# Token mixing of one encoder layer in a new order on all engines, with some products in unsplit float32

## The chip, the cores and the metric

The kernel runs on one core of a Trainium2 chip: TensorE (matrix products into PSUM), VectorE (DVE in the profile), ScalarE (ACT), GpSimd (POOL), SyncE (SP, whose queue issues nearly all loads here), and 16 DMA engines that bring data from HBM into SBUF. The metric is device time in microseconds, the median of several runs; lower is better.

## What is computed

One layer for 256 tokens of width 1024, in float32:

```python
z = x @ w_in + b_in                        # 1024 -> 2304: pool 256, q, k, v 512 each, conv a, g 256 each
mix = concat(pool_mixer(z), neighbourhood_attention(z), conv_module(z)) @ w_out + b_out
x1 = layer_norm(ALPHA * x + mix, ln1_g, ln1_b)
logits = x1 @ w_router + b_router          # 32 experts, the top 4 of each token, softmax over them
for e in range(32):
    g = minimum(x1 @ w_gate[e] + b_gate[e], 7.0)
    u = clip(x1 @ w_up[e] + b_up[e], -7.0, 7.0)
    out += gates[:, e:e+1] * (((u + 1) * g * sigmoid(1.702 * g)) @ w_down[e] + b_down[e])
y = layer_norm(ALPHA * x1 + out, ln2_g, ln2_b)
```

The pool mixer takes centred means over 2, 4, 8 and 16 tokens; attention runs over a 4 by 64 grid in 2 x 16 query blocks with a learned bias; the conv module is GLU, a depthwise convolution of 31 taps, a layer norm over 256 channels, swish and a 256 x 256 product. Each expert has three 1024 x 1024 float32 matrices, 12.6 MB, so the expert weights are 403 MB.

## The kernel before, in words

Everything is one function, `encoder_layer`, in a schedule written out by hand: each engine executes its instructions in the order of the text, and semaphores for data and buffers are added by the framework. The loads go through one in-order queue (SP).

**Buffers.** 22 slots of 128 x 2048 float32 (1.05 MB), `slot(i, name)`; a tile in a slot waits until everything that used the tile before it is done. In token mixing they hold the input x transposed (slot 0), the raw input weights (`wi`), their split parts (`wp`), q and k, the attention scores (`sb`), W_out raw and split (`wo`). As they come free, `load_ahead` (line 307) fills them with expert 0's weights in the order of `places`, and in the loop over experts `load_expert(e + 1)` (line 895) loads the next expert's 12 pieces in the same cycle of 20 places. PSUM: four accumulator banks `acc` (2 halves of tokens x 2 halves of channels), three rotating banks `bk` and one `bg`.

**Split products.** A float32 operand is written as the sum of a rounded high part (`nc.scalar.copy` into float32r) and a low part (raw minus high, on VectorE, or on GpSimd where `eng=nc.gpsimd`), line 104. `zstep` (line 213) then makes three float32r products, high x high, high x low, low x high. `zproj` does this for 8 slices of the 1024 channels and four 128-column blocks: first the conv columns, then Q, K, pool, V.

**Order of token mixing.** Loads of x and the conv columns in eight pieces; conv, Q; the taps of the depthwise convolution (62 VectorE instructions, `run_taps`) fill VectorE's gaps; K; pool columns (`wi_p`); scores with mask and bias (lines 353 to 363: VectorE scales and adds, takes the maximum, negates it, ScalarE makes the exponentials); nine pooling steps on GpSimd (lines 328 to 336); V; normalisation of the scores (line 391); transposes of probabilities and V (415, 420), pool columns through their map (405), attention products (434). GpSimd also subtracts for half of V's split (107) and all four parts of W_out (299), adds the mask to the bias table (201), and splits the gate and up biases into three bfloat16 parts (470, 636).

**Output projection and norm 1.** `outproj(tt, kk)` (line 476) adds slice kk of the mix for token half tt to two accumulators, three split products each. Between them stand the conv module's layer norm (488 to 509; its two products with the reciprocal deviation are line 508), its pointwise product (520), and x times ALPHA plus b_out (501). Then norm 1 by token halves: `stats1` adds (572) and takes statistics, `ln_stats` ends in a power on GpSimd (551), `apply1` scales on VectorE (577), `turn1` transposes the normed rows and applies the gain (583, 561, 563), `router` multiplies by the router weights (598) and finds the top 8, `chosen` and `positions` make a mask and each token's place in its expert's list, `acc_start` (592) puts ALPHA times x1 into the four accumulators.

**Experts.** Each has 64 places. `gather` (716) picks its tokens with a 0/1 matrix (`slots_of`, 707) for two experts at a time, `first` (748) makes the gate and up products, `act_gate`, `act_up` (768) the activation, `turn` (778) transposes, `down` (801) the third product, `scatter` (813) adds the gated rows to the accumulators one expert later, `select` (695) prepares the scatter matrix. The fullest expert has more tokens than 64: `places_of` (984) exchanges its column with that of expert `FULL` = 16 in small tables (`exchange`, 999 to 1008, six times), and at `e == FULL` a second block of 32 places is computed (`block`, with the gather of line 727). The order of expert weights is read at run time from `whose`. After expert 31 the second norm is done and stored.

## Time and profile before

| | us |
|---|---|
| median of 3 runs | 1088.27 (1087.99 to 1088.78) |
| the profiled execution | 1080.62 |
| its span, first to last instruction | 1078.4 |
| TensorE busy in the span | 975.7 (90%) |
| VectorE | 333.4 (31%) |
| ScalarE | 167.6 (16%) |
| GpSimd | 77.4 (7%) |
| DMA: bytes moved, mean rate | 422.99 MB, 392 GB/s |

A share over the whole span mixes the first 175 us, where the layer's first half runs, with 900 us of experts; the rows below are of single stages. A float32 product leaves two records of TensorE, a float32r or bfloat16 product or a transpose one. "PEclk" is the share of the full TensorE clock that was granted, 1.00 for 2.4 GHz and 0.50 for 1.2.

### The profile page before, as it was taken

Reading aid. Unit: us, or ns where it says so; the run is one execution under the profiler, and the core shown is the slowest. Engines: PE = TensorE matmul, PEld = TensorE weight load, DVE = VectorE, ACT = ScalarE, POOL = GpSimd, SP = SyncE. Lnnn points to the kernel's source line nnn. Section 1 sums busy time; section 2 is a strip of 40 time slices with the busy share of each in tenths; the row PEclk is TensorE's granted clock in tenths of the full one; section 3 lists DMA queues with packets and bytes.
Section 4 is the critical chain, followed back from the end, with each engine's and each line's share of the span. In section 5 each row is a group of like instructions: output and inputs, shape, how many; then the busy total and the mean of one; then the engine's idle time right before and its main releaser. Section 6 shows DMA issues by size and latency. Waiting matters only on the chain.

```text
span 1078.4 us, 13697 instructions
## 1 busy us (share of the span) xinstructions
PE 975.7 (90%) x5194; PEld 424.3 (39%) x5194; DVE 333.4 (31%) x795; ACT 167.6 (16%) x331; POOL 77.4 (7%) x40
## 2 busy tenths in 40 slices
PE   7968889999999999998989899999989898898985
PEld 6956734343434343433324343433223232323222
DVE  5999652222212322221221312222112121212114
ACT  5644411011101010100101110101001010101001
POOL 1894200000000000000000000000000000000001
PEclk9989889999999999999999999999999999999998
DMA  9674779999999999999999999999999999999994
GB/s 340 265 308 169 310 282 393 421 421 421 421 421 422 421 421 421 421 421 421 421 421 421 420 420 421 422 421 421 420 421 422 421 421 421 420 422 420 421 401 171
DMA packets 61768, 422.99 MB, mean 392 GB/s; under 512 B 6818, under 2 KB 7330, under 8 KB 11780
## 3 DMA queue, kind: packets, MB, share of 16 engines
q1 hardware_dynamic: 61348, 421.42, 95.2%
q8 instruction: 42, 0.69, 0.3%
q0 software_dynamic: 208, 0.40, 0.1%
q10 hardware_dynamic: 144, 0.26, 0.1%
q14 instruction: 26, 0.21, 0.0%
HBM read 421.01 MB, written 1.05 MB: 391 GB/s over the span
## 4 chain that ended last, share of the span: by engine, by line
DMA 69%; PE 19%; DVE 6%; issue 3%; POOL 1%; ACT 1%; SPq 0%; DVEq 0%; ACTq 0%; POOLq 0%
DMA w<-in_w_up_dram 23%; DMA w<-in_w_down_dram 23%; DMA w<-in_w_gate_dram 22%; PE bk L748 5%; PE bk L801 4%; PE bg L748 3%; PE bk L716 1%; DVE cacc L255 1%; DVE sb L391 1%; PE acc L482 1%; DVE more L508 1%; DMA wi<-in_w_in_dram 0%; PE bk L778 0%; PE acc L218 0%; ACT wp L106 0%
## 5 line engine op out<-in xcount | busy, mean ns | idle before, releaser
L748 PE MATMUL bk<-w,xgp 128*64 128x512 f32 x1024 | 240.2, 603 | 21.1 <-DMA w<-in_w_up_dram 21.0
L748 PE MATMUL bg<-w,xgp 128*64 128x512 f32 x1024 | 231.4, 595 | 17.6 <-DMA w<-in_w_gate_dram 17.6
L801 PE MATMUL bk<-w,aT 128*64 128x512 f32 (+1 forms) x1024 | 226.4, 598 | 1.2 <-DMA w<-in_w_down_dram 1.2
L748 PEld LDWEIGHTS bg<-w,xgp 128*64 128x64 f32 x1024 | 70.7, 136 | 167.5 <-issue 111.1
L748 PEld LDWEIGHTS bk<-w,xgp 128*64 128x64 f32 x1024 | 67.5, 137 | 162.9 <-issue 101.7
L801 PEld LDWEIGHTS bk<-w,aT 128*64 128x64 f32 (+1 forms) x1024 | 69.3, 136 | 135.7 <-issue 127.2
L806 DVE SCALAR_TENSOR_TENSOR y<-bk,gs,y 128x512 fp32r<-128x512 f32 x31 | 23.3, 751 | 272.9 <-ACT y L805 272.9
L757 DVE TENSOR_SCALAR g<-bg 128x512 f32<-128x512 f32 x32 | 22.1, 691 | 175.3 <-PE bg L748 175.3
...
L780 ACT COPY aT<-bk 128x256 f32<-128x256 f32 (+1 forms) x66 | 24.4, 369 | 262.0 <-PE bk L778 257.5
L758 ACT ACTIVATE s<-g 128x512 f32<-128x512 f32 (+1 forms) x33 | 20.6, 624 | 261.8 <-DVE g L757 261.8
L716 PE MATMUL bk<-se,xa 128*128 128x128 f32 x512 | 59.9, 275 | 0.0
L716 PEld LDWEIGHTS bk<-se,xa 128*128 128x128 f32 x512 | 58.4, 192 | 0.0
L768 DVE TENSOR_SCALAR u<-bk 128x256 f32<-128x256 f32 (+1 forms) x66 | 27.5, 417 | 95.6 <-PE bk L748 95.6
L805 ACT ACTIVATE y<-bk,gs 128x512 fp32r<-128x512 f32 x31 | 21.3, 687 | 214.3 <-PE bk L801 214.3
L813 PE MATMUL acc<-y,st 64*128 64x512 f32 x248 | 46.4, 447 | 1.1 <-ACT y L805 0.8
L778 PE MATMUL bk<-ident,g 128*128 128x128 f32 x128 | 27.7, 299 | 15.0 <-DVE g L769 14.1
L698 DVE TENSOR_SCALAR st<-bk 128x256 fp32r<-128x256 f32 x32 | 13.6, 425 | 81.2 <-PE bk L695 81.2
L216 PE MATMUL acc<-x,wp 128*128 128x256 f32 x96 | 29.1, 303 | 7.6 <-ACT wp L106 7.6
L561 ACT ACTIVATE xgp<-bk,g1b 128x128 f32<-128x128 f32 x64 | 24.1, 458 | 76.0 <-PE bk L716 76.0
L563 DVE TENSOR_SCALAR xgp<-bk,g1b 128x128 f32<-128x128 f32 x64 | 21.9, 404 | 44.1 <-PE bk L716 44.1
L218 PE MATMUL acc<-x,wp 128*128 128x256 f32 x96 | 29.1, 303 | 4.5 <-POOL wp L107 4.0
...
## 6 DMA issues: line engine op xcount, KB each, us to landing
...
w<-in_w_down_dram SPq DMA_DIRECT2D x124, 1024.0 KB, 19.8
wi<-in_w_in_dram SPq DMA_DIRECT2D x7, 1024.0 KB, 11.6
...
```

The lines of the kernel that those rows point to most:

```text
L216: nc.tensor.matmul(b[:, :256], w(0, k, j), xh[:, k, :], start=(k == 0), stop=False)
L218: nc.tensor.matmul(b[:, :256], w(1, k, j), xh[:, k, :], start=False, stop=(k == 7))
L561: nc.scalar.activation(o, i, AF.Identity, bias=b, scale=g)
L716: nc.tensor.matmul(p[:, i * 128:(i + 1) * 128], x1n[:, tt, (g + i) * 128:(g + i) * 128 + 128], se[:, tt, :], start=(tt == 0), stop=(tt == 1))
L748: nc.tensor.matmul(p[i * c:(i + 1) * c, :n], xg[:, k, :], w[k // 2][:, k % 2, i * n:(i + 1) * n], start=False, stop=(k == 7))
L757: nc.vector.tensor_scalar(g[:], p[:, :n], 7.0, None, op0=ALU.min)
L768: nc.vector.tensor_scalar(u[:, o], p[:, o], -7.0, 7.0, op0=ALU.max, op1=ALU.min)
L778: nc.tensor.transpose(p[:, j * 128:j * 128 + 128], a[:, j * 128:j * 128 + 128], ident[:])
L780: nc.scalar.copy(aT[:, o], p[:, :h * 256].rearrange("p (j n) -> p j n", n=128)[:, o])
L801: nc.tensor.matmul(p[o:o + c, :], aT[:, k % h, k // h * c:(k // h + 1) * c], rows_of(w, k, dh), start=(k == of_part[0]), stop=(k == of_par ...
L806: nc.vector.scalar_tensor_tensor(y[:, 1], p[:], gs[:], y[:, 0].bitcast(F32), op0=mult, op1=sub)
L813: nc.tensor.matmul(acc[tt][dh][:], st[dh * 64:dh * 64 + 64, tt, :], y[dh * 64:dh * 64 + 64, i, :], start=False, stop=False, skip_group_che ...
```

## The change

Token mixing is ordered anew:

- The conv columns and the pool columns of the input projection are float32 products from the raw weights (`zplain`, one float32 product instead of three float32r ones); Q, K and V stay split. So do W_out's slices 2 to 7, while its slices 0 and 1 (pool rows, `WHOLE`) are unsplit float32 products.
- All splits, the masks and the pooling steps run on VectorE. GpSimd keeps the broadcasts of bias rows, the powers of the layer norms, and the issue of twelve small loads within SBUF that put the three parts of the gate and up biases in place (`bias_parts`); the biases come as one array of 128 partitions. The negation of the maxima is made by the reduction. V's evacuation is all on ScalarE.
- Loads: x and the conv columns come in five pieces; slots are dealt out differently (`places`); x itself is loaded before the weights of expert 0.
- The router's products are made from the rows before norm 1 (`hT`, `scores`): router weights times the gain (`gw`), and mean and deviation of each row are applied to the 32 scores (`rsum`). Norm 1's scaling runs on ScalarE. The top-4 mask is made by one comparison and one reduction.
- ALPHA times x1 isn't put into the accumulators before the experts; `add_x1` adds one of its four quarters in each of the experts 4, 6, 10 and 12.
- Expert 0's tokens are gathered alone, expert 1's within expert 0's up product. Of the exchange of columns only `whose` is made before expert 0, the other tables after its up product. The exchanged place is expert 20 instead of 16.

The diff, cut to its core:

```diff
-FULL = 16
+FULL = 20
+X1_AT = (4, 6, 10, 12)
...
+    for t, src, o in ((xT, xT_d, slice(0, 2)), (wi_conv[0], w_in_at[1792], slice(0, 2)), (xT, xT_d, slice(2, 8)),
+                      (wi_conv[0], w_in_at[1792], slice(2, 4))):
+        nc.sync.dma_start(t[:, o, :], src[:, o, :])
+    nc.sync.dma_start(wi_conv[1], w_in_at[1792][:, 4:8, :])
...
-    wi_k = load_in(768, 512, (1, 2))
+    wi_k = load_in(768, 512, (13, 19))
+    wi_p = load_in(0, 256, (14,))
...
-    nc.gpsimd.dma_start(bgu[:, 0], b_gate)
-    nc.gpsimd.dma_start(bgu[:, 1], b_up)
-    nc.gpsimd.dma_start(small[32:33, :D], rows_d[:, :D])
-    nc.gpsimd.dma_start(small[64:65, :32], rows_d[:, D:D + 32])
-    nc.gpsimd.dma_start(bdn, b_down)
+    bgu = small[:, :512]
+    bparts = small[:, 512:1280].bitcast(BF16).rearrange("p (i f) -> p i f", i=3)
+    nc.sync.dma_start(bgu, b_gu)
+    brows = small[:, 1280:1792]
+    for i in range(2):
+        nc.sync.dma_start(brows[32 + 32 * i:33 + 32 * i, :], rows_d[:, i * 512:i * 512 + 512])
+    nc.sync.dma_start(brows[96:97, :32], rows_d[:, D:D + 32])
+    nc.sync.dma_start(bdn, b_down)
+    wi_v = load_in(1280, 512, (1, 2))
...
-        nc.gpsimd.tensor_tensor(biasT[:, pair, :, :124], biasT[:, pair, :, :124],
+        nc.vector.tensor_tensor(biasT[:, pair, :, :124], biasT[:, pair, :, :124],
...
+    def bias_parts():
+
+        for i in range(3):
+            if i:
+                nc.vector.tensor_tensor(bgu, bgu, bparts[:, i - 1], op=sub)
+            nc.scalar.copy(bparts[:, i], bgu)
+            for h in range(2):
+                for m in range(2):
+                    p = 64 * h + 32 * m
+                    nc.gpsimd.dma_start(bg3[32 * i:32 * i + 32, m, h * 512:h * 512 + 512], bparts[p:p + 32, i])
+
+    def zplain(raw, bs):
+
+        per = 8 // len(raw)
+        for k in range(8):
+            for j, b in enumerate(bs):
+                nc.tensor.matmul(b[:, :256], raw[k // per][:, k % per, j * 128:j * 128 + 128], xT[:, k, :],
+                                 start=(k == 0), stop=(k == 7))
...
+    zplain(wi_conv, bks)
+    act_table(AF.Sigmoid)
+    for i in range(0, 8, 4):
+        split(xT[:, i:i + 4], xh[:, i:i + 4], xl[:, i:i + 4])
     wp_q.add(wi_q[0], (9, 10))
     wp_q.add(wi_q[1], (11, 12))
-    wi_p = load_in(0, 256, (4,))
-    load_bias(1)
-    wi_v = load_in(1280, 512, (3,))
-    wi_v += load_in(1280, 512, (13,), 1)
-    bks = [acc[i // 2][i % 2] for i in range(4)]
-    act_table(AF.Sigmoid)
-    zproj(wp_c, bks)
+    qbs = [bank("bg" if j == 3 else "bk") for j in range(4)]
+    zproj(wp_q, qbs)
+    wp_k.add(wi_k[0], (5, 6))
...
-    NT = (4, 12, 3, 9, 16, 4, 3)
+    TAPS = (8, 10, 16, 8, 100, 14)
...
+    run_taps(TAPS[0])
+    wp_v.add(wi_v[0], (9, 10))
+    wp_v.add(wi_v[1], (11, 12))
+    run_taps(TAPS[5])
+    add_mask(1)
...
-    wo_raw = {k: load_rows(p, w_out, k) for k, p in ((1, 1), (2, 2), (0, 19), (3, 3))}
-    wo_places = ((0, 14), (5, 6), (7, 8), (11, 12))
+    bias_parts()
+    wo_raw = {k: load_rows(p, w_out, k) for k, p in ((1, 21), (0, 3), (2, 4), (3, 13))}
+    xa = slot(19, "xa")[:].rearrange("p (t d) -> p t d", t=2)
+    nc.sync.dma_start(xa, x_d.rearrange("p (t d) -> p t d", t=2))
+    WHOLE = (0,)
+    wo_places = ((5, 6), (7, 8), (1, 2), (9, 10))
     wo = {}
 
-    def split_out(k, eng=nc.gpsimd):
+    def split_out(k):
 
         hi, lo = [slot(p, f"wo{p}", F32R)[:].rearrange("p (k c) -> p k c", k=2) for p in wo_places[k]]
         wo[k] = hi, lo
-        nc.scalar.copy(hi, wo_raw[k])
-        return lambda: eng.tensor_tensor(lo, wo_raw[k], hi.bitcast(F32), op=sub)
-
-    places = (21, 13, 1, 9, 10, 15, 16, 2, 5, 6, 3, 7, 8, 0, 14, 11, 12, 18, 4, 17)
+        assert k not in WHOLE
+        split(wo_raw[k], hi, lo)
+
+    places = (5, 6, 0, 15, 16, 21, 4, 11, 12, 3, 13, 7, 8, 1, 2, 18, 14, 9, 10, 17)
...
+    zplain(wi_p, pbs)
...
-        nc.vector.tensor_reduce(mx[:, i0:i0 + 4], t, axis=AX.X, op=ALU.max)
-        nc.vector.tensor_scalar(mx[:, i0:i0 + 4], mx[:, i0:i0 + 4], -1.0, None, op0=mult)
+        nc.vector.tensor_reduce(mx[:, i0:i0 + 4], t, axis=AX.X, op=ALU.max, negate=True)
...
+    nc.vector.tensor_tensor(s2[:, :, 1:272], uT[:, :, 0:271], uT[:, :, 1:272], op=add)
+    nc.vector.tensor_tensor(s4[:, :, 1:271], s2[:, :, 0:270], s2[:, :, 2:272], op=add)
...
+    split_out(1)
+    split_out(2)
...
+        if kk // 2 in wo:
+            wh, wl = [w[:, kk % 2] for w in wo[kk // 2]]
+            ps = (mh, wh), (mh, wl), (ml, wh)
+            ps = [(a[:, kk], w) for a, w in ps]
+        else:
+            ps = [(more[:, kk // 6, kk % 2], wo_raw[kk // 2][:, kk % 2])]
...
+    run_taps(TAPS[2])
     pool_out()
+    load_ahead(5)
+    for tt in range(2):
+        outproj(tt, 0, first=True)
+    run_taps(TAPS[3])
...
+    split_out(3)
...
+    gw = pa.tile([128, 8, 64], F32, name="gw", tag="cacc")
+    rsum = pa.tile([128, 64], F32, name="rsum")
+    wr = par[:, P_WR:P_WR + 256].rearrange("p (k e) -> p k e", k=8)
+    for i, p in enumerate((P_G1, P_B1)):
+        nc.vector.tensor_tensor(gw[:, :, 32 * i:32 * i + 32], wr, par[:, p:p + 8, None].to_broadcast([128, 8, 32]), op=mult)
...
+            nc.scalar.activation(half(tt, dh), half(tt, dh), AF.Identity, bias=shift[:], scale=mv[:, 1:2])
...
+        nc.vector.scalar_tensor_tensor(lg[:], rsum[:, :32], mv[:, 0:1], b[:, :32], op0=mult, op1=add)
+        nc.vector.scalar_tensor_tensor(lg[:], lg[:], mv[:, 1:2], rsum[:, 32:], op0=mult, op1=add)
...
+        eq = pa.tile([128, 4, E], F32, name=f"eq{tt}", tag="sig")
+        nc.vector.tensor_tensor(eq[:], i32[:, None, :].to_broadcast([128, 4, E]),
+                                i8[:, :4, None].to_broadcast([128, 4, E]), op=ALU.is_equal)
+        nc.vector.tensor_reduce(msk[:, tt], eq[:].rearrange("p j e -> p e j"), axis=AX.X, op=add)
...
+    turn1(0, 0, nc.scalar)
+    turn1(0, 1, nc.scalar)
     for kk in (6, 7):
         outproj(1, kk, (1,), last=(kk == 7))
+    stats1(1, 0)
+    l0 = scores(0)
+    turn1(1, 0, nc.scalar)
     stats1(1, 1)
+    turn1(1, 1, nc.scalar)
     mv1 = ln_stats(pa, st1[:, 1], "a1")
+    apply1(0, mv0)
+    *r0, i0 = router(0, l0, mv0)
+    chosen(0, i0)
+    l1 = scores(1)
     apply1(1, mv1)
-    *r0, f0 = router(0)
-    acc_start(0, (0,))
-    turn1(1, (nc.scalar, nc.vector))
-    bias_part(2)
-    acc_start(0, (1,))
-    chosen(0, f0)
-    *r1, f1 = router(1)
-    chosen(1, f1)
+    *r1, i1 = router(1, l1, mv1)
     positions(0)
-    acc_start(1, (0,))
+    chosen(1, i1)
     positions(1)
...
+    def add_x1(tt, dh):
+
+        p = bank()
+        t = wk.tile([128, 512], F32, name="x1T", tag="ax", bufs=1)
+        for c in range(4):
+            o = slice(c * 128, c * 128 + 128)
+            nc.tensor.transpose(p[:, o], x1n[:, tt, dh * 512 + c * 128:dh * 512 + c * 128 + 128], ident[:])
+            affine(nc.scalar, t[:, o], p[:, o], 4 * dh + c)
+
+        def rest():
+            for c in range(4):
+                o = slice(c * 128, c * 128 + 128)
+                nc.tensor.matmul(acc[tt][dh][:, o], t[:, o], aid[:], start=False, stop=False, skip_group_check=True)
+
+        return rest
...
         exchange(whose[:], i32[:1], 1)
+        yield
...
+    gather(slots_of([of(posm, 0)]), xgp[:, 0, :, :CAP], CAP)
     counts()
-    gather(se, xgp[:, 0])
+    exchanges = places_of()
+    next(exchanges)
+    gates(0, *r0)
+    gates(1, *r1)
     act_table(AF.Sigmoid)
-    places_of()
+    se = slots_of([of(posm, 1)])
...
+            if e in X1_AT:
+                i = X1_AT.index(e)
+                later.append(add_x1(i // 2, i % 2))
+            if e == 0:
+                got.append(select(sg))
+                sg1 = pick(of(pos1, 1), of(gate1, 1))
+                gather(se, xgp[:, 0, :, CAP:], CAP)
+                got.append(select(sg1))
+            elif e + 1 < E:
...
+        act_up(first(sel, 1, xg, W[1], between=(4, ahead)), g)
         if e == 0:
-            st = select(pick(of(pos, 0), of(gate, 0)))
-            sg = pick(of(pos1, 1), of(gate1, 1))
-        act_up(first(sel, 1, xg, W[1], between=(4, ahead)), g)
+            st = got[0]
+            list(exchanges)
         if 0 < e < E - 1:
-            scatter(*pend, (0,))
+            scatter(*pend, (0,), start=(e == 1))
+        for f in later:
+            f()
```

## Rows read from the trace of the kernel before

**Rows 1.** The page: the span, and one of the small loads.

```profile
span 1078.4 us, 13697 instructions
...
small<-in_b_gate_dram POOLq DMA_DIRECT2D x1, 128.0 KB, 7.3
```

**Rows 2.** Stages: stage, length, busy of each engine, PEclk, DMA share, GB/s.

```profile
0.00:50.00 50.00, 41.92 (x328) 41.63 (x329) 38.43 (x67) 29.55 (x31) 20.73 (x11) 1.00 0.86 326
50.00:100.00 50.00, 38.46 (x323) 33.62 (x322) 47.43 (x66) 25.64 (x68) 35.16 (x16) 0.86 0.62 240
100.00:150.00 50.00, 40.36 (x222) 30.29 (x220) 37.30 (x119) 18.97 (x34) 14.63 (x7) 0.93 0.72 273
150.00:175.00 25.00, 21.63 (x92) 7.32 (x94) 6.82 (x21) 2.06 (x4) 0.00 (x0) 0.86 0.84 319
175.00:1040.00 865.00, 809.39 (x4118) 302.14 (x4116) 189.95 (x501) 87.66 (x189) 0.00 (x0) 1.00 1.01 421
```

**Rows 3.** The chain of work: start, duration, what.

```profile
172.03 6.87 PE bg L748 x32
...
224.08 6.87 PE bg L748 x32
...
262.71 19.75 DMA w<-in_w_down_dram
...
606.63 1.05 PE bk L727 x16
...
624.25 1.21 PE acc L813 x7
```

**Rows 4.** The timeline of the SP queue: start, duration, line, loads.

```profile
141.91 5.48 SPq L140 DMA_DIRECT2D w<-in_w_down_dram  x4
156.59 6.19 SPq L140 DMA_DIRECT2D w<-in_w_gate_dram  x4
```

**Rows 5.** The timeline of GpSimd.

```profile
38.15 19.90 POOL L107 TENSOR_TENSOR wp<-wi,wp 128x2048 fp32r<-128x2048 f32 x1 [2.34 <-ACT wp L106]
...
60.28 4.60 POOL L299 TENSOR_TENSOR wo<-w,wo 128x2048 fp32r<-128x2048 f32 x1
```

**Rows 6.** The timeline of VectorE.

```profile
39.28 2.28 DVE L107 TENSOR_TENSOR wp<-wi,wp 128x2048 fp32r<-128x2048 f32 x1
...
53.59 0.66 DVE L358 SCALAR_TENSOR_TENSOR sb<-bk,biasT 128x496 f32<-128x496 f32 x1
...
70.80 8.59 DVE L391 TENSOR_TENSOR sb<-sb,rs 128x496 f32<-128x496 f32 x4
...
101.75 6.39 DVE L508 TENSOR_TENSOR more<-more,std 128x256 f32<-128x256 f32 x2
...
125.36 0.69 DVE L572 TENSOR_TENSOR xa<-acc,xa 128x512 f32<-128x512 f32 x1 [1.97 <-PE acc L482]
...
162.45 0.42 DVE L768 TENSOR_SCALAR u<-bk 128x256 f32<-128x256 f32 x1 [2.84 <-PE bk L748]
```

**Rows 7.** The chain of work in the first 140 us.

```profile
13.77 0.12 PE acc L216
...
32.89 1.58 ACT qk L278 x4
...
89.24 5.69 PE acc L482 x24
94.92 0.88 PE bk L488 x4
...
136.15 3.67 PE bk L716 x32
```

**Rows 8.** The timeline of ScalarE.

```profile
45.86 1.91 ACT L298 CAST wo<-w 128x2048 fp32r<-128x2048 f32 x1
...
58.51 0.38 ACT L363 ACTIVATE sb<-sb,mx 128x124 f32<-128x124 f32 x1
...
68.69 3.13 ACT L379 ACTIVATE vB<-acc,par 128x124 f32<-128x124 f32 x12
```

263 lines of the change are left out of this document (101 added, 162 removed).

## The prediction

> **What bounds the kernel now.** I read the page's span first, then busy time by stage, then the chain of work, then the queue that issues loads, and last the engines one by one over the first 165 us. The profiled execution takes 1080.62 us around a span of 1078.4 [rows 1]; it lies 7.65 below the median of 1088.27, and I take a shift worked out in it as a shift of the median.
>
> By stage [rows 2] the DMA rings carry 421 GB/s from 175 us to 1040, and the chain of work there is mostly weight loads, each behind the one before, as the row at 262.71 [rows 3]. Expert weights are 384 pieces of 128x2048 float32, 1.05 MB, 12 to an expert: 12.6 MB / 421 GB/s = 29.9 us an expert. TensorE takes less: the gate products of experts 1 and 3 start at 172.03 and 224.08, so two experts take 52.05 us, 26.0 each. From some expert on the end is set by when the load stream last stood still, plus what is left to carry. So only idle DMA time at the start matters. The stages [rows 2] give 326x50 + 240x50 + 273x50 + 319x25 = 49.9 MB by 175 us, where 421 would have carried 73.7: 23.8 MB, or **56 us, are lost**. No ordering can win more.
>
> Why does the stream stand still? Twenty buffers of 1.05 MB hold weights, and all serve token mixing first. The SP queue is in order, so each load waits for the last reader of its buffer. Experts 0 and 1 need 24 pieces; the last four of expert 1 are issued while expert 0's gate product lets buffers go, and expert 2's gate weights only from 156.59 on, behind expert 0's up product [rows 4]. The time at which token mixing and expert 0 are done is therefore what the change can move.
>
> **The change part by part.**
> *GpSimd's elementwise work goes.* The same 128x2048 subtraction took GpSimd 19.90 us at 38.15 and 4.60 at 60.28 [rows 5]; VectorE takes 2.28 [rows 6]. And VectorE itself is long beside it: four normalisations of 128x496 took 8.59 us, where the 128x496 op of the scores took 0.66 [rows 6]; two 128x256 products took 6.39, where each should be under that 0.66, 1.3 together. Clean, the two steps cost 2.6 and 1.3, so 11 us of VectorE go; the negations go into the reduction, and norm 1's scaling goes to ScalarE. The Trainium skill (GPSIMD Engine Reference, 8. Key points) says that GpSimd shares its SBUF interfaces with VectorE and contends with it; by that rule the long rows end with GpSimd's work; 19.90 against 4.60 agrees with it, and if it did not hold the second rival would be the forecast. VectorE takes over: the V split 2.3, three W_out splits 6.8, nine pooling ops on up to 542 columns, some 4.5, two masks 2.3, bias 1.4, router weights 0.8: 18 us, against the splits of conv and pool columns (three times 2.28, worked as four halves and one whole) and the 11 us. Net VectorE does about as much without the gaps, and nothing on it waits for GpSimd but two small powers.
>
> *TensorE's path, worked forward.* A float32r product of 128x256 takes one record of 0.12 us, three to a split product; a float32 one two of 0.22 [rows 7]. Before, Q was done at 32.89 [rows 7] after 192 records, 23.0 us: 9.9 went to the first loads, casts and a half clock. I keep it whole. Conv: 64 records x 0.22 = 14.1: 24. Unsplit costs 2.6 more TensorE time than 96 x 0.12; the dropped wait for casts, under 2, I don't count. Q and K, 96 records each, 11.5 each: 47. Pool columns 32 x 0.22: 54. Scores 3.5: 57. V 11.5: **69**. Before, V ended at 68 to 70 as well: ScalarE's evacuation of it starts at 68.69 [rows 8]; its weights had waited on GpSimd's 19.9. Here no gain yet.
>
> Now ScalarE leads: 16 exponentials x 0.38, two W_out casts of 1.9, 16 evacuations of V at 3.13/12 = 0.26 [rows 8], eight PSUM copies of 512 columns near 0.5 (a quarter of 1.91), two pool evacuations: 6.1 + 3.8 + 4.2 + 4 + 0.9 = 19 us from 57, so 76. VectorE has scores (8 ops, 5.5), pooling 4.5, normalisation 2.6 and two splits behind it, done by 70, off the path. Half of the pool rows' output products (8 unsplit, two records of 0.43 each, 6.9 in all) stand ahead of the attention products (under 4): attention ends near 83. Before, its products ended and the output projection began at 89.24 [rows 7]. **Gain 6.**
>
> Output projection: W_out rows 2 to 7 are 72 records of 5.69/24 = 0.24, 17; channel sums 1.8, the pointwise product 1.8, router sums 1.8, the other pool-row half 3.4, and 1 to 3 of waits (the reciprocal chain now has splits and products queued over it, not the 6.39 row): 110. Before, the last addition of norm 1 came at 125.36 [rows 6]. **Gain 15.** Behind the 6.39 row's stall the next thing late is ScalarE's swish, 1 us.
>
> Norm 1 to the first gate product: before 125.36 to the end of the gather at 136.15 + 3.67 = 139.8 [rows 6, 7], 14.5. After: addition 0.7, four transposes 0.6, copy 0.6, router 8 products 1.8, VectorE's eight small rows 1.8 (0.22 each, where 256 columns take 0.42 [rows 6]), positions 0.5, selection 0.5, gather of 16 products x 2 x 0.115 = 3.7, evacuation 1.4: 11.6. Start of gate **122**, gain 18. The statistics and the scaling of the rows run beside the router, since scores are scaled afterwards.
>
> Expert 0: before, VectorE has the whole exchange of columns queued ahead of the gate's result, and up, which could end two products of 7.1 after 139.8, ends at 162.45 [rows 6], 8.5 late. After, the exchange of job numbers alone comes first. Gate 7.1 (6.87 [rows 3] and its bias), up 7.1 with selection and the second gather inside (0.7 + 3.7), 1 us of waits: **141**, gain 21. The rest of the exchange (31 small rows, under 7) follows on VectorE behind expert 0's up; it is first needed for expert 2's selection, in expert 1.
>
> *Clock.* The granted clock is 0.86, 0.93 and 0.86 in the stages from 50 to 175 [rows 2]: 14 + 7 + 7 us at half speed. TensorE's waits are fewer after; I keep 2 to 3 us of that cost on the path. **Shift 19.**
>
> *The DMA side agrees.* Loads before expert weights are some 18.3 MB; with 20 pieces 39.3 MB, 93 us; the first 50 us lost 11 [rows 2], of which I keep 8. Buffers 15 and 16 wait for V's end at 69 (10 us idle), 11 and 12 for attention (4), 13 for its split (3), 18 for the projection's end (4), some 2 each of latency behind them: 122 to 126 until the twentieth piece landed. Idle 31 to 37 instead of 56: 19 to 25.
>
> *At nothing:* bias parts by twelve small loads on GpSimd's queue, wanted from 122 on: one of before landed in 7.3 us [rows 1], cover 60. VectorE's two bias subtractions wait for ScalarE's copies behind K's evacuation, with ten taps and the scores behind; they end 3 us before the scores want VectorE; without that cover up to 3. V's loads wait for conv's products at 24, behind 11 MB of other loads that keep the rings busy past 30. Adding x1 in four later experts is 4 transposes and 8 records each, under 2 us of TensorE against 3.9 of slack an expert. The Trainium skill (DMA: Bandwidth & Descriptors, Bandwidth) has transfers under 64 KB dominated by descriptors; the twelve loads are 32 KB. By it they would take longer, and still the cover would do.
>
> **The rivals.**
> 1. *More waits than I count.* ScalarE's 19 us stage grows, or TensorE falls to half clock again in the gaps at 72 and around the router: two stretches more cost 3 to 7 of the 28 us above. Gain 12: **1076**. For it: ScalarE is in order and serves softmax, casts and V.
> 2. *The long VectorE rows are the ops' own*, so the change doesn't take away what it should: normalisation 6 and products 5.1 longer, 11 together, all on the path: gain 8, **1080**. Against it: 4.60 and 19.90 for one op show that durations there depend on the neighbour.
> 3. *More gain:* the 21 above keeps its 2 to 3 of clock and loses the 4 to 6 of waits counted in: 27, **1061**.
> 4. *Slower: TensorE ends behind the loads.* The fullest expert's second block (606.63 to 624.25 + 1.21, 18.8 us [rows 3]) moves from expert 16 to 20, and x1 adds 7. With 3.9 us an expert it is made up in five experts, by 26. It decides only if TensorE's period after expert 20 reaches 29.9; then the backlog of 19 to 25 stays at the end and eats the gain: **1091**.
>
> **How the numbers follow.** 1088.27 - 19 = 1069. Chances: forecast 0.60, rival 1 0.16, rival 2 0.09, rival 3 0.10, rival 4 0.03, no effect 0.02. The range of 1060 to 1080 takes in rivals 1 to 3 with their bounds. About 0.2% is what a measurement of this kernel can tell from no change; faster 0.95, same 0.02, slower 0.03.
>
> **What would show it.** Right: no long VectorE row before 120, GpSimd nearly empty, expert 0's gate at 118 to 126, its up ending 138 to 145, DMA at 421 from 145 on. Wrong: rows of VectorE over 2 us at the normalisation, ScalarE gapless from 57 to 85, a low clock around the router, or TensorE waiting for no load after expert 26.

## The result, and the profile after

The changed kernel takes **1060.2 us** (median; 1058.84 to 1061.21), the kernel before 1088.53 beside it: a ratio of 0.974, with an interval of 0.9723 to 0.9756. That is 28.3 us less; 19 were forecast. The profiled execution of after takes 1060.73 us around a span of 1058.9, so it lies at the median. The profiled execution of before lay 7.65 below its own. Between the two profiles the difference is 19.5 us (1078.4 - 1058.9), which is the forecast. The other 8.8 us are the question of the first experiment.

The head of the page of after (as [rows 1]), with the line of busy time, in which GpSimd is down to 2%:

```profile
span 1058.9 us, 13693 instructions
...
PE 986.5 (93%) x5202; PEld 431.9 (41%) x5202; DVE 307.0 (29%) x791; ACT 161.7 (15%) x339; POOL 16.3 (2%) x28
```

The stages of after, in the columns of [rows 2]:

```profile
0.00:50.00 50.00, 44.24 (x277) 41.20 (x278) 29.16 (x49) 19.85 (x22) 2.51 (x8) 1.00 0.97 389
50.00:100.00 50.00, 47.69 (x374) 38.51 (x373) 45.21 (x86) 31.15 (x81) 5.86 (x11) 1.00 0.69 260
100.00:150.00 50.00, 46.34 (x244) 29.07 (x244) 26.86 (x120) 11.33 (x24) 1.15 (x2) 0.86 0.81 319
150.00:175.00 25.00, 24.59 (x134) 10.78 (x132) 7.83 (x25) 3.57 (x8) 0.00 (x0) 1.00 1.00 410
175.00:1020.00 845.00, 797.82 (x4054) 302.36 (x4052) 184.77 (x489) 92.04 (x198) 0.00 (x0) 0.99 1.01 421
```

389x50 + 260x50 + 319x50 + 410x25 gives 58.7 MB by 175 us, where before had 49.9 [rows 2] and 421 GB/s would have carried 73.7. The 15.0 MB still missing are 35.7 us of idle rings; the forecast's DMA side had 31 to 37. The 8.7 MB gained are 20.7 us, the whole difference of the spans within 1.2.

VectorE in after, the rows that answer to [rows 6] (start, duration, line, operation):

```profile
65.17 2.43 DVE L394 TENSOR_TENSOR sb<-sb,rs 128x496 f32<-128x496 f32 x4
71.92 9.59 DVE L277 SCALAR_TENSOR_TENSOR cacc<-hp,par,cacc 128x256 f32<-128x256 f32 x24
...
93.10 0.76 DVE L510 TENSOR_TENSOR more<-more,std 128x256 f32<-128x256 f32 x2
...
106.39 0.69 DVE L586 TENSOR_TENSOR xa<-acc,xa 128x512 f32<-128x512 f32 x1 [0.43 <-PE acc L436]
...
143.28 0.42 DVE L781 TENSOR_SCALAR u<-bk 128x256 f32<-128x256 f32 x1 [2.06 <-PE bk L761]
```

The normalisation is 2.43 where it was 8.59, the two products 0.76 where they were 6.39. The last addition of norm 1 stands at 106.39 (before 125.36), the first half of expert 0's up result at 143.28 (before 162.45).

TensorE in after from the end of the router to expert 0's gate, in the same columns, and expert 1's gate:

```profile
113.06 0.41 PE L635 MATMUL bk<-msk,cst 128*128 128x32 f32 x2 [1.44 <-DVE msk L628]
114.00 7.06 PE L729 MATMUL bk<-se,xa 128*128 128x64 f32 x32 [0.54 <-DVE se L720]
...
122.22 9.65 PE L761 MATMUL bg<-w,xgp 128*64 128x512 f32 x32
...
152.62 7.04 PE L761 MATMUL bg<-w,xgp 128*64 128x512 f32 x32
```

Expert 0's gate takes 9.65 where expert 1's takes 7.04. The gather ahead of it and its own first 5.2 us ran at half clock (1.2 GHz): the granted clock is 0.50 from 113.8 to 127.4. TensorE had stood still for 1.44 and 0.54 us just before.

The loads on the SP queue, in the columns of [rows 4]:

```profile
125.89 6.36 SPq L141 DMA_DIRECT2D w<-in_w_down_dram  x4
133.86 9.74 SPq L141 DMA_DIRECT2D w<-in_w_gate_dram  x4
```

Expert 2's gate weights are issued from 133.86 on, 22.7 us earlier than before [rows 4].

### The profile page after: what moved, and what is told of

Read it like the earlier page. It is cut to its first block, busy times and chain, and to the rows that moved or that the text cites. A ratio compares the mean times of both kernels' runs of the same rounds, so it can differ in the third digit from the quotient of the medians.

```text
span 1058.9 us, 13693 instructions
## 1 busy us (share of the span) xinstructions
PE 986.5 (93%) x5202; PEld 431.9 (41%) x5202; DVE 307.0 (29%) x791; ACT 161.7 (15%) x339; POOL 16.3 (2%) x28
## 4 chain that ended last, share of the span: by engine, by line
DMA 51%; PE 42%; DVE 3%; ACT 2%; issue 1%; SPq 0%; DVEq 0%; ACTq 0%
DMA w<-in_w_up_dram 18%; DMA w<-in_w_down_dram 16%; DMA w<-in_w_gate_dram 13%; PE bk L761 11%; PE bk L814 10%; PE bg L761 9%; PE bk L729 4%; PE acc L436 2%; DMA cst<-in_cst_dram 2%; DMA wi<-in_w_in_dram 2%; PE acc L826 1%; PE bk L791 1%; DVE cacc L277 1%; ACT sb L358 1%; PE bk L708 1%
## 5 line engine op out<-in xcount | busy, mean ns | idle before, releaser
L761 PE MATMUL bg<-w,xgp 128*64 128x512 f32 x1024 | 233.8, 603 | 11.2 <-DMA w<-in_w_gate_dram 11.1
L729 PE MATMUL bk<-se,xa 128*128 128x128 f32 (+1 forms) x544 | 66.8, 284 | 0.5 <-DVE se L720 0.5
L729 PEld LDWEIGHTS bk<-se,xa 128*128 128x128 f32 x544 | 65.3, 200 | 0.6 <-issue 0.6
L771 ACT ACTIVATE s<-g 128x512 f32<-128x512 f32 (+1 forms) x33 | 20.6, 625 | 250.7 <-DVE g L770 250.7
L781 DVE TENSOR_SCALAR u<-bk 128x256 f32<-128x256 f32 (+1 forms) x66 | 27.5, 417 | 93.6 <-PE bk L761 93.6
L791 PE MATMUL bk<-ident,g 128*128 128x128 f32 x128 | 27.6, 298 | 13.6 <-DVE g L782 12.4
L577 DVE TENSOR_SCALAR xgp<-bk,g1b 128x128 f32<-128x128 f32 (+1 forms) x68 | 22.7, 397 | 51.6 <-PE bk L729 51.6
L575 ACT ACTIVATE xgp<-bk,g1b 128x128 f32<-128x128 f32 (+1 forms) x68 | 25.1, 450 | 82.0 <-PE bk L729 82.0
L711 DVE TENSOR_SCALAR st<-bk 128x256 fp32r<-128x256 f32 x32 | 13.6, 425 | 82.3 <-PE bk L708 82.3
L826 PEld LDWEIGHTS acc<-y,st 64*128 64x128 f32 x248 | 19.1, 186 | 32.0 <-issue 29.5
L772 DVE TENSOR_TENSOR g<-g,s 128x512 f32<-128x512 f32 (+1 forms) x33 | 22.6, 684 | 24.6 <-ACT s L771 24.6
L791 PEld LDWEIGHTS bk<-ident,g 128*128 128x128 f32 x128 | 13.3, 143 | 37.5 <-issue 22.4
```

The lines of the kernel that those rows point to most:

```text
L575: nc.scalar.activation(o, i, AF.Identity, bias=b, scale=g)
L577: eng.tensor_scalar(o, i, g, b, op0=mult, op1=add)
L729: nc.tensor.matmul(p[:, i * n:(i + 1) * n], x1n[:, tt, (g + i) * 128:(g + i) * 128 + 128], se[:, tt, :], start=(tt == 0), stop=(tt == 1))
L761: nc.tensor.matmul(p[i * c:(i + 1) * c, :n], xg[:, k, :], w[k // 2][:, k % 2, i * n:(i + 1) * n], start=False, stop=(k == 7))
L772: nc.vector.tensor_tensor(g[:], g[:], s[:], op=mult)
L781: nc.vector.tensor_scalar(u[:, o], p[:, o], -7.0, 7.0, op0=ALU.max, op1=ALU.min)
```

## The experiments

Twelve runs were made, in three groups; each group had its own runs of the kernel before beside it (medians 1088.4, 1087.8 and 1087.1).

One number ties them together. From the start of expert 0's down product to the end of the span lie 913.7 us in before and 913.4 in after. If the load stream alone counts from there on, this number stays, and an edit is worth what it moves that start by:

| kernel | expert 0's down product starts | span | from there to the end |
|---|---|---|---|
| before | 164.73 | 1078.4 | 913.7 |
| before, profiled again | 173.36 | 1086.0 | 912.6 |
| before, without GpSimd's elementwise work | 152.89 | 1065.9 | 913.0 |
| after | 145.49 | 1058.9 | 913.4 |
| after, elementwise work back on GpSimd | 147.11 | 1060.4 | 913.3 |
| after, joint gather and whole exchange | 146.07 | 1058.3 | 912.2 |
| after, norm 1 ahead of the router | 154.65 | 1067.6 | 913.0 |
| after, x1 ahead of expert 0 | 161.78 | 1075.3 | 913.5 |
| after, second block after expert 16 | 145.46 | 1058.7 | 913.2 |
| after, TensorE kept busy | 139.48 | 1053.5 | 914.0 |
| after, TensorE kept busy, joint gather | 138.59 | 1052.3 | 913.7 |
| after, convolution split | 145.33 | 1063.2 | 917.9 |
| the same, TensorE kept busy | 139.63 | 1057.6 | 918.0 |
| after, x1 in experts 1 to 4 | 145.41 | 1061.8 | 916.4 |

In eleven rows the last column is 912.2 to 914.0. The three at the foot lose 3 to 5 us more behind that start; they are taken up below.

### The kernel before once more

No edit.

> Nothing is changed: this is the kernel before, profiled and timed once more. The profiled execution of before took 1080.62 us, its timed runs 1088. Theory A: the 7.65 us between them are TensorE's clock or a load stream that differs from execution to execution; then this profile lies anywhere from 1080 to 1089, and if it lies near 1088 its idle DMA time before 175 us is about 8 us more than 56 (3 MB less carried), and the place is seen. Theory B: a profiled execution of this kernel is always some 8 us shorter than a timed one; then this profile is again at 1080 to 1081 with 49.9 MB by 175 us.

Measured: 1088.93, with the profile at a span of 1086.0. **Theory A holds.** In all, 47 timed executions of the kernel before fall into two groups with nothing between: ten took 1077.1 to 1080.8, thirty-seven 1086.5 to 1090.9. The trace on which the prediction rests is one of the short kind. The stages of the long kind, against [rows 2], and rows of GpSimd, VectorE and TensorE:

```profile
0.00:50.00 50.00, 39.37 (x306) 38.87 (x307) 38.47 (x51) 28.23 (x29) 15.91 (x13) 1.00 0.96 365
50.00:100.00 50.00, 30.15 (x313) 28.11 (x312) 48.38 (x72) 23.44 (x64) 24.62 (x15) 0.80 0.43 172
```

```profile
37.90 4.71 POOL L107 TENSOR_TENSOR wp<-wi,wp 128x2048 fp32r<-128x2048 f32 x1 [5.52 <-ACT wp L106]
```

```profile
38.05 4.85 DVE L255 SCALAR_TENSOR_TENSOR cacc<-hp,par,cacc 128x256 f32<-128x256 f32 x1
...
60.71 17.84 DVE L255 SCALAR_TENSOR_TENSOR cacc<-hp,par,cacc 128x256 f32<-128x256 f32 x16
78.48 0.66 DVE L358 SCALAR_TENSOR_TENSOR sb<-bk,biasT 128x496 f32<-128x496 f32 x1
```

```profile
87.79 1.08 PE L415 MATMUL bk<-ident,sb 128*124 128x128 f32 x4 [19.83 <-ACT vB L379]
```

The same program runs with the opposite winner. VectorE in the short kind, from the trace of [rows 6]:

```profile
38.09 1.26 DVE L255 SCALAR_TENSOR_TENSOR cacc<-hp,par,cacc 128x256 f32<-128x256 f32 x3
...
47.25 6.42 DVE L255 SCALAR_TENSOR_TENSOR cacc<-hp,par,cacc 128x256 f32<-128x256 f32 x16
...
54.99 3.08 DVE L361 TENSOR_SCALAR mx<-mx 128x4 f32<-128x4 f32 x1
```

In the short kind a tap of the convolution began at 38.09, 0.06 us ahead of GpSimd's split at 38.15 [rows 5]. The taps kept their usual length (three took 1.26, sixteen 6.42), and the split took 19.90: it ended 4.4 us after the last of the sixteen. In the long kind GpSimd's split begins at 37.90, 0.15 ahead of the tap. The split takes 4.71, and the tap 4.85, until just after the split's end. The sixteen taps take 17.84 there, beside GpSimd's pooling and splits: half of them still take no more than 0.47 each, the longest 4.78. So single taps wait out whole operations of GpSimd. One trace of each kind was read; that all executions of a group share its order is likely from their times, and not shown.

The taps stand in VectorE's queue ahead of the scores, so the scores come at 78.48 instead of 53.59 [rows 6], and TensorE stands still for 19.83 us. The stream then has 172 GB/s from 50 to 100 where the short kind had 240, and by 175 us 46.9 MB against 49.9: 3.0 MB, 7.1 us of the 7.65.

The Trainium skill (SBUF — State Buffer, Who interferes with whom) says that the shared port pair is held for a whole instruction and that issue order, not the shape of an operation, decides who blocks. Both traces agree: the operation that began first, by 0.06 or 0.15 us, kept its length, and the other one waited. By the same section a VectorE operation with at most one SBUF input, outside the modes with two ports, doesn't contend; here too the rows agree, since the scores, which read PSUM and one SBUF tile, take 0.66 in either trace, at 53.59 in the midst of GpSimd's split [rows 5, 6].

### GpSimd's elementwise work taken away from the kernel before

```diff
-        nc.gpsimd.tensor_tensor(biasT[:, pair, :, :124], biasT[:, pair, :, :124],
+        nc.vector.tensor_tensor(biasT[:, pair, :, :124], biasT[:, pair, :, :124],
...
-    wp_v.add(wi_v[0], (9, 10), nc.gpsimd)
+    wp_v.add(wi_v[0], (9, 10))
...
-    def split_out(k, eng=nc.gpsimd):
+    def split_out(k, eng=nc.vector):
...
-    nc.gpsimd.tensor_tensor(s2[:, :, 1:272], uT[:, :, 0:271], uT[:, :, 1:272], op=add)
+    nc.vector.tensor_tensor(s2[:, :, 1:272], uT[:, :, 0:271], uT[:, :, 1:272], op=add)
...
```

> The kernel before with one part of the change alone: every elementwise operation of GpSimd ahead of the experts (half of V's split, three W_out splits, pooling, masks, the bias subtractions) is issued to VectorE at the same place of the program; order, loads, experts and exchange stay. Theory: the contention ends, so the normalisation rows fall from 8.59 to 2.6, the two products from 6.39 to 1.4, V's low half from 19.90 to 2.3; VectorE does 17 us more, of which 11 are paid by the shorter rows. Between those the kernel gains 6 to 12: 1076 to 1082, and no VectorE row over 2.4 stands before 120 us. Rival: the long rows belong to those operations and VectorE is only loaded further (47 of 50 us busy from 50 to 100): 1088 to 1100, with the rows of 8.6 and 6.4 still there.

Measured: **1067.74** (1066.61 to 1067.87), 20.6 below the 1088.4 beside it, ratio 0.9835 (0.9771 to 0.9899). The theory's mechanism holds, and its size was too small: it was sized on the short kind. Against that kind's span the gain is 12.5 (1078.4 to 1065.9). VectorE of this kernel:

```profile
51.63 6.42 DVE L255 SCALAR_TENSOR_TENSOR cacc<-hp,par,cacc 128x256 f32<-128x256 f32 x16
...
64.77 0.67 DVE L358 SCALAR_TENSOR_TENSOR sb<-bk,biasT 128x496 f32<-128x496 f32 x1
...
74.78 2.43 DVE L391 TENSOR_TENSOR sb<-sb,rs 128x496 f32<-128x496 f32 x4
...
99.44 0.76 DVE L508 TENSOR_TENSOR more<-more,std 128x256 f32<-128x256 f32 x2
```

All rows are short although VectorE now does everything, and the scores come 13.7 us earlier than in the long kind (64.77 against 78.48). Its four executions lie within 1.3 us; since 37 of 47 of before lie in one group, four alike don't show that the second kind is gone. Moving a few operations from one engine to another, in place, is worth 20.6 of the 28.3 against the median of before.

### Elementwise work put back on GpSimd in the changed kernel

```diff
-    wp_v.add(wi_v[0], (9, 10))
+    wp_v.add(wi_v[0], (9, 10), nc.gpsimd)
...
-    split_out(1)
-    split_out(2)
+    split_out(1, nc.gpsimd)
+    split_out(2, nc.gpsimd)
...
-    nc.vector.tensor_tensor(s2[:, :, 1:272], uT[:, :, 0:271], uT[:, :, 1:272], op=add)
+    nc.gpsimd.tensor_tensor(s2[:, :, 1:272], uT[:, :, 0:271], uT[:, :, 1:272], op=add)
...
```

> The changed kernel with elementwise work put back on GpSimd: half of V's split, the low parts of two of W_out's row blocks, and the nine pooling operations; everything else as changed. Theory: each 128x2048 subtraction takes GpSimd between 4.6 and 20 us, VectorE's rows beside it grow again (normalisation over 4 in all, where it is 2.43), attention's end moves from 83 us to 90 to 98, and the kernel gives back 7 to 15 of its gain: 1067 to 1075. Rival: the gain came from the order, the unsplit columns and the router; GpSimd's work has cover in the new order: 1060 to 1063, with short VectorE rows.

Measured: 1063.09 (1062.18 to 1063.57), 2.9 above after. The rows are the theory's, and the time is the rival's within 0.1. GpSimd and VectorE of this kernel:

```profile
36.86 4.64 POOL L108 TENSOR_TENSOR wp<-wi,wp 128x2048 fp32r<-128x2048 f32 x1 [36.44 <-ACT wp L107]
```

```profile
64.10 6.85 DVE L394 TENSOR_TENSOR sb<-sb,rs 128x496 f32<-128x496 f32 x4
70.87 13.85 DVE L277 SCALAR_TENSOR_TENSOR cacc<-hp,par,cacc 128x256 f32<-128x256 f32 x24
```

The contention is back: normalisation 6.85 instead of 2.43, twenty-four taps 13.85 instead of 9.59. But in the new order the taps that suffer stand behind the normalisation, not ahead of the scores. The gather starts 3.2 us later than in after, at 117.23, and half of that comes back because gather and gate run at half clock for less long (6.72 and 8.40 us against 7.06 and 9.65). Expert 0's down product starts 1.6 us later, at 147.11. So taking GpSimd's work away gains 20.6 in the old order, and putting three pieces of it back costs 2.9 in the new. The pieces are not all the same (the masks, the third split of W_out and the bias parts stay on VectorE here). That the price is a matter of what is queued behind the operation that is slowed is therefore argued from these rows, and not shown by the two times alone.

### The router behind norm 1 again

```diff
+    apply1(0, mv0)
     turn1(0, 0, nc.scalar)
...
     stats1(1, 1)
-    turn1(1, 1, nc.scalar)
     mv1 = ln_stats(pa, st1[:, 1], "a1")
-    apply1(0, mv0)
+    apply1(1, mv1)
+    turn1(1, 0, nc.scalar)
+    turn1(1, 1, nc.scalar)
...
-        nc.vector.scalar_tensor_tensor(lg[:], rsum[:, :32], mv[:, 0:1], b[:, :32], op0=mult, op1=add)
-        nc.vector.scalar_tensor_tensor(lg[:], lg[:], mv[:, 1:2], rsum[:, 32:], op0=mult, op1=add)
+        nc.vector.tensor_tensor(lg[:], b[:, :32], rsum[:, 32:], op=add)
```

> The changed kernel with one part undone, the router ahead of norm 1: rows are normalised before they are transposed, and the router's scores come from the normalised rows. Theory: per block of tokens the power on GpSimd (0.55), the shift and ScalarE's scaling (2 x 0.83) come between the last addition and the transposes: gather 2.5 to 5 us later than at 114, and TensorE stands still longer, so that half clock begins earlier: 1062 to 1067. Rival: these steps find cover under the output projection's last products, gather at 114 to 115.5: 1059 to 1062.

Measured: **1068.62** (1066.71 to 1069.84), 8.4 above after: the theory's direction, and more than its price. TensorE:

```profile
107.96 1.36 PE L598 MATMUL bk<-ident,xa 128*128 128x128 f32 x8 [2.37 <-ACT xa L593]
...
115.48 1.82 PE L598 MATMUL bk<-ident,xa 128*128 128x128 f32 x8 [1.48 <-ACT xa L593]
...
131.49 9.55 PE L760 MATMUL bg<-w,xgp 128*64 128x512 f32 x32
```

The two waits for ScalarE's scaling are 3.9 us. The rest goes with the clock: the granted clock is 0.50 from 116 to 136.5 and mostly so from 109 to 112.5, so that scores, gather and gate ran at half speed, and longer than in after. Expert 0's gate starts 9.3 us later than in after.

### x1 ahead of expert 0 again

```diff
     counts()
+    for i in range(4):
+        add_x1(i // 2, i % 2)()
...
-            if e in X1_AT:
-                i = X1_AT.index(e)
-                later.append(add_x1(i // 2, i % 2))
```

> The changed kernel with one part undone, x1 added to the sums in later experts: all 16 transposes and 16 products with the scaled identity stand ahead of expert 0's gate product. Theory: the gate starts 5 us (full clock) to 10 us (half clock) later, at 127 to 133, and the load stream stands still as much longer: 1064 to 1070; the 7 us that experts 4, 6, 10 and 12 get back are worth nothing. Rival: the products keep TensorE at work and shorten the stretch at half clock, so that half the price comes back: 1061 to 1063.

Measured: **1078.89** (1077.1 to 1081.15), 18.7 above after, twice the theory's highest price. TensorE, from the first product with the scaled identity to expert 0's gate:

```profile
123.46 1.92 PE L841 MATMUL acc<-aid,x1T 128*128 128x128 f32 x8
...
138.62 1.92 PE L841 MATMUL acc<-aid,x1T 128*128 128x128 f32 x8
...
140.89 7.28 PE L761 MATMUL bg<-w,xgp 128*64 128x512 f32 x32
```

The four blocks follow each other every 5.05 us, because each transpose waits for ScalarE to empty the bank of the one before (0.55 to 0.61 us each). That is this placement's own price; the kernel before had these products between the router's waits. What the run does show is the rate of exchange. The gate starts 18.7 us later than in after (140.89 against 122.22) and takes 7.28 where after's takes 9.65, so expert 0's down product starts 16.3 later (161.78 against 145.49), and the span of the same execution, the fastest of ten, is 16.4 longer (1075.3 against 1058.9).

### x1 in the next four experts

```diff
-X1_AT = (4, 6, 10, 12)
+X1_AT = (1, 2, 3, 4)
```

> The changed kernel with x1 added in experts 1, 2, 3 and 4, not 4, 6, 10 and 12: one size changed, nothing left out. Theory: once expert 0 runs, only the load stream counts; its period is 29.9 us an expert, TensorE's 26, and 2 to 4 us more in an expert have cover: 1059 to 1062. Rival: the chain of work of the changed kernel follows TensorE up to some 447 us, so loads wait for TensorE there, and what the four additions cost comes at the end: 1065 to 1072.

Measured: 1062.57 (1061.06 to 1063.65), 2.4 above after, between the two. Expert 0 is as early as in after, but the stream now stands still behind it. Two stages of this kernel:

```profile
175.00:200.00 25.00, 23.29 (x116) 8.77 (x114) 4.55 (x10) 3.89 (x8) 0.00 (x0) 1.00 0.97 382
...
225.00:250.00 25.00, 23.57 (x123) 12.35 (x125) 5.00 (x13) 4.31 (x10) 0.00 (x0) 0.93 0.99 397
```

The rings carry 382 and 397 GB/s there, where after carries 420 and 421: together 1.6 MB, 3.7 us. From expert 0's down product to expert 4's TensorE takes 121.6 us (145.41 to 267.01), 30.4 an expert, and the stream's own period is 29.9. After takes 109.0 for the same four (145.49 to 254.48). So TensorE, not the stream, is late in the first experts, and work added there is paid for, and more dearly than in experts 4, 6, 10 and 12.

### The exchange in one piece

```diff
-    gather(slots_of([of(posm, 0)]), xgp[:, 0, :, :CAP], CAP)
+    gather(slots_of([of(posm, 0), of(posm, 1)]), xgp[:, 0])
...
-    next(exchanges)
     gates(0, *r0)
     gates(1, *r1)
+    list(exchanges)
...
-                gather(se, xgp[:, 0, :, CAP:], CAP)
...
-            list(exchanges)
```

> The changed kernel with one part undone, the split of the exchange: tokens of experts 0 and 1 are gathered together ahead of expert 0's gate product, and the whole exchange of columns with the gates stands on VectorE ahead of expert 0. Theory: expert 0's gate starts some 3.5 to 7 us later (16 more products in the gather, at half clock), its up product waits for VectorE's 31 small rows, and up's end moves from 145 to 148 to 152, with the loads behind it: 1063 to 1067. Rival: the gather is only moved out of expert 0's up product and the exchange has cover under the gate product: 1059 to 1062.

Measured: 1059.01 (1058.17 to 1060.14), 1.2 below after: the rival. TensorE:

```profile
115.78 5.36 PE L729 MATMUL bk<-se,xa 128*128 128x128 f32 x32 [0.70 <-DVE se L720]
...
121.68 7.03 PE L761 MATMUL bg<-w,xgp 128*64 128x512 f32 x32
...
136.68 0.73 PE L708 MATMUL bk<-ident,sg 128*128 128x128 f32 x2 [2.64 <-DVE sg L699]
137.34 6.41 PE L761 MATMUL bk<-w,xgp 128*64 128x512 f32 x16
```

The wait for VectorE behind the exchange is there (1.09 and 2.64 for the two selections), and it brings half clock into the up product (6.41 for sixteen records where 3.65 is usual). But the gather for both experts took 5.36 where after's for one took 7.06, because the clock came back after 3.4 us, and the second gather inside expert 0 fell away. Gain and loss cancel: expert 0's down product starts at 146.07 against 145.49. Splitting the exchange was worth nothing by itself.

### TensorE kept busy at the end of the router

```diff
+    def keep_busy(n):
+        nc.tensor.matmul(bank("bg")[:, :n], onesm[:], par[:, :n], start=True, stop=True)
...
+        if tt == 1:
+            keep_busy(512)
+            keep_busy(256)
         nc.tensor.matmul(b[:, :32], tri, msk[:, tt], start=(tt == 0), stop=True)
+        if tt == 1:
+            keep_busy(256)
```

> The changed kernel with three products that no result uses put into TensorE's idle time at the end of the router: 512 and 256 float32 columns ahead of the last product of the positions (1.44 us idle there), 256 columns behind it (0.54 idle). In the changed kernel TensorE falls to half clock from 114 to 127.5 us, and the gather takes 7.06 us where 3.6 is its time at full clock, expert 0's gate 9.44 where 7.1. Theory: the fall comes from the 2 us of idleness from 111.6 to 114; filled, the clock stays, the gather ends 3.5 us earlier and the gate 5 to 6 us earlier, and with them the load stream: 1053 to 1057. Rival: the fall comes from the small products of the router ahead of it (32 columns each and transposes from 106 to 111.6), which stay: half clock as before, and the added products cost 0 to 1: 1060 to 1062.

Measured: **1056.29** (1055.33 to 1057.25), 3.9 below after; between the profiles 5.4. TensorE:

```profile
111.36 1.86 PE L631 MATMUL bg<-par,onesm 128*128 128x512 f32 x4
...
113.28 0.70 PE L631 MATMUL bg<-par,onesm 128*128 128x256 f32 x2
114.49 3.76 PE L737 MATMUL bk<-se,xa 128*128 128x64 f32 x32 [0.51 <-DVE se L728]
...
118.84 7.04 PE L769 MATMUL bg<-w,xgp 128*64 128x512 f32 x32
...
157.52 3.74 PE L737 MATMUL bk<-se,xa 128*128 128x128 f32 x32
```

The theory holds: the granted clock is 1.00 through this stage, the gather takes 3.76 instead of 7.06, the gate 7.04 instead of 9.65, and it ends 6.0 us earlier. The last row is the gather for experts 2 and 3, with 128 columns. Six records of work that nobody needs make the kernel faster.

### The same, with one gather for experts 0 and 1

```diff
-    gather(slots_of([of(posm, 0)]), xgp[:, 0, :, :CAP], CAP)
+    gather(slots_of([of(posm, 0), of(posm, 1)]), xgp[:, 0])
...
-                gather(se, xgp[:, 0, :, CAP:], CAP)
```

> The run with three products that no result uses at the end of the router, and one thing more: tokens of experts 0 and 1 are gathered together ahead of expert 0's gate product (the exchange stays split, its larger part behind expert 0's up product). There a gather of 128 columns took 3.74 us where one of 64 columns took 3.76, so that the second gather inside expert 0's up product, 3.68 us, is TensorE time for nothing. Theory: expert 0's gate starts within 0.5 us of where it did, up ends 3.3 to 3.7 earlier, and the end comes 3 to 4 us earlier: 1052 to 1053.5, the fastest so far. Rival: up's end then waits for VectorE's selections, or the loads wait for something else than expert 0: 1055 to 1057.

Measured: **1055.09** (1054.13 to 1055.58), 1.2 below the run before it and the fastest kernel of the study; ratio to before 0.9724 (0.9658 to 0.9790). Nearer the rival. TensorE:

```profile
110.80 3.29 PE L631 MATMUL bg<-par,onesm 128*128 128x512 f32 x4
...
127.04 3.60 PE L769 MATMUL bk<-w,xgp 128*64 128x512 f32 x16
...
132.11 0.59 PE L716 MATMUL bk<-ident,sg 128*128 128x128 f32 x2 [1.10 <-DVE sg L707]
132.62 3.65 PE L769 MATMUL bk<-w,xgp 128*64 128x512 f32 x16
```

Without the gather between the halves of the up product, the second selection waits 1.10 us for VectorE, and only some 2 of the 3.68 us come back. And here the clock was at half for 3.4 us from 110.9 on, ahead of the gap that the three products fill (the four records took 3.29, where they took 1.86 in the run above). TensorE had been busy for 1.80 of the 1.80 us before that, with products of 32 columns. So filling the gap ended the long stretch of after, but the gap isn't the whole cause of a fall. Up to the gather the two kernels give TensorE the same instructions, and the clock fell in one profile and not in the other; one profile of each doesn't show how often it does.

### The convolution's columns split again

```diff
-    zplain(wi_conv, bks)
+    for i in range(0, 8, 2):
+        split(xT[:, i:i + 2], xh[:, i:i + 2], xl[:, i:i + 2])
+        o = slice(i % 4, i % 4 + 2)
+        split(wi_conv[i // 4][:, o], wp_c.v[i // 4][0][:, o], wp_c.v[i // 4][1][:, o])
+    zproj(wp_c, bks)
...
```

> The changed kernel with the convolution's columns split again into two parts (96 short products on parts, as in the kernel before), not float32 unsplit (64 records of 0.22 us). Theory: TensorE's first product waits for ScalarE's cast (7.3 us instead of 5.8) but needs 11.5 us instead of 14.1, so that the convolution's columns are done within 1 us of the changed kernel's 22.2; ScalarE and VectorE have four more casts of about 1.2 us each there, and the time stays at 1059 to 1062: this part of the change is worth nothing by itself. Rival: those casts push back the splits of Q and K, and TensorE stands still between them: 1063 to 1067.

> The convolution's columns split again, with the three products that no result uses at the end of the router. The run with the split columns alone took 1065.2, though its load stream and its TensorE stood within 0.3 us of the changed kernel's up to 1018 us; there TensorE stopped for 5.2 us ahead of the last expert's gate product, while an instruction load stood in the queues. Theory: those 5 us belong to where the instruction stream is cut and not to the split; with twelve instructions more the cut moves, and the time is that of the run with the three products: 1055 to 1058. Rival: the split itself costs 5: 1060 to 1063.

Measured: 1065.19 (1064.96 to 1067.47), 5.0 above after, and with TensorE kept busy 1059.32 (1057.81 to 1062.6), 3.0 above the run without the split. Up to the last expert both are level with their partners: expert 0's down product starts at 145.33 and 139.63 against 145.49 and 139.48, and the last expert's gate weights are issued within 0.5 us of each other. TensorE at the last expert's gate, in after, then in the one and in the other:

```profile
1018.57 0.64 PE L755 MATMUL bg<-bg,bselp 96*64 96x512 bf16 x2 [0.28 <-PEq L984]
```

```profile
1024.40 8.97 PE L765 MATMUL bg<-w,xgp 128*64 128x512 f32 x32 [5.20 <-DMA w<-in_w_up_dram]
```

```profile
1018.90 0.64 PE L767 MATMUL bg<-bg,bselp 96*64 96x512 bf16 x2 [6.19 <-PEq L996]
```

So the split costs nothing where it stands (K's columns even leave PSUM at 42.9 instead of 44.6), and 3 to 5 us near the end, where TensorE comes out of the branch of the late loop: it stands still for 5.20 and 6.19 us, where after waits 0.28 us. In both runs queues that carry instructions move 8 and 16 KB in just these windows, and the second stop is ended by TensorE's own sequencer. The profile puts the first down to a load of up weights, which this gate product doesn't read. That TensorE waits for its program there, and that the cut of the program into such loads decides whether it does, is argued and not shown: after has such loads near this place too, 24 KB between 1018.6 and 1027. The theory that twelve instructions more would remove the stop fell: it came back at the same place.

### The second block after expert 16 again

```diff
-FULL = 20
+FULL = 16
```

> The changed kernel with the fullest expert's second block after expert 16 as in the kernel before, not 20. Theory: TensorE has caught up with the loads by then in both places, 1059.5 to 1061.5. Rival: at 16 TensorE is still behind (its lead over the loads grows by 3.9 us an expert and the block takes 18.8), loads wait for it once: 1063 to 1070.

Measured: 1060.2 (1057.86 to 1061.45), the median of after to the digit. The theory holds.

## Why the prediction held, and what it missed

**What bounds the kernel: right.** In eleven of the fourteen profiles only the time at which the load stream runs without gaps counted: the last column of the table above is constant within 1.8 us over them, while their ends lie 34 us apart. The other three lose 3 to 5 us more behind it.

**The base: the step that failed.** "I take a shift worked out in it as a shift of the median." The 7.65 us between profile and median were named and then passed over. They were the second kind of execution of the kernel before, which is 8 us longer and makes up 37 of 47, and which none of after's four executions shows; they lie within 2.4 us. Against the short kind the change gains 17 to 21 us, which is the forecast of 19; against the median it gains 28. That the time still lies inside the stated range is luck in part: it is 0.2 us above the lower edge, and two of the four executions lie below it.

**GpSimd's work: right in kind, too small in size.** The forecast had 11 us of VectorE in two long rows, and took the 19.90 as a sign of who suffers. In the usual execution those two rows are short, 2.43 and 0.76, and VectorE suffers most in the taps (17.84 against 6.42 for sixteen), which no row of the short kind showed. So the mechanism was right, and its place was that of one execution in five. With this part alone the kernel gains 20.6. The second rival (the long rows are the operations' own) fell: the same operations take 2.43 and 0.76 in the kernel before without GpSimd's work.

**TensorE's path forward, term by term.** Convolution done at 24: ScalarE reads it at 22.2. K at 47: its evacuation starts at 44.6. (The half clock counted ahead of Q stands in no granted clock, which is 1.00 from 0 to 50 [rows 2]; the trace of before has TensorE's records 0.21 us apart up to 13.5 and 0.12 from there.) V's end at 69: 66.7, with its evacuation from 65.45 on. Attention's end at 83: the last row of its split is at 83.48. Last addition of norm 1 at 110: 106.39; the 1 to 3 us of waits added there didn't come, since TensorE is busy for 36.67 of the 37 us from 74 to 111. Gate start at 122: **122.22**, but by two errors that cancel: 3.6 us early into the router, and 3.5 us lost in the gather, 7.06 for 3.6. Up's end at 141: 143.3, behind a gate product of 9.65 where 7.1 was counted.

**Clock.** "I keep 2 to 3 us of that cost on the path" was too little by about 2 to 3: the run with TensorE kept busy prices the stretch from 113.8 to 127.4 at 5.4 us of span. That is the second place of the first rival ("around the router"), which so came true while the forecast did too, because the waits it was paired with stayed out. The sign that would have shown the forecast wrong, a low clock around the router, was there. ScalarE's stage was no rival: V's evacuation, the copies and the pool evacuations behind it end at 74.2, where 76 was forecast.

**The exchange.** That expert 0's up ends "8.5 late" behind VectorE was read rightly from before, and the change ends it. But the run with the exchange in one piece lies 1.2 us below after, with executions that overlap: that part could have stayed as it was, since the second gather inside expert 0 costs as much as the wait that it avoids.

**The router ahead of norm 1** stood in the sum only as 14.5 us that become 11.6. Undone alone it costs 8.4: 3.9 are waits for ScalarE's scaling, and the clock is at half for 20.5 us at a stretch, where after's is for 13.6.

**Float32 unsplit, FULL and x1: at nothing, rightly,** for the convolution's columns where they stand and for FULL, and nearly so for x1: in experts 1 to 4 it costs 2.4 us more than in 4, 6, 10 and 12. The claim behind it, 3.9 us of slack in an expert, does not hold for the first ones, in which loads wait for TensorE. Its price, "under 2 us of TensorE", was too small: in after a quarter lengthens TensorE's time for an expert by 3.2 to 4.9 us (29.1 and 27.5 from one down product to the next, where 24.2 is usual without a gather), with three of its four transposes behind ScalarE. No run puts back the split of the pool columns or of W_out's first slices, or the old order of loads and slots; their shares stay open.

**Rival 3** gave 1061 and the time is 1060.2, but not on its grounds: the waits that it left out did stay out, while the clock cost more, and 8 of the 28 us are the base. **Rival 4** was not seen: moving the second block changes nothing, and from 777.92 to 1042.8 after's chain is loads alone, one behind the other.

Three runs that put one part back (contention 2.9, router 8.4, x1 in a place of its own 18.7) and the one that takes one part alone (20.6) add up to far more than 28.3. The parts are not terms of a sum: each is worth what it moves the start of expert 0's down product by, given what else stands ahead of it.
